# A Deltanet / RWKV-7 layer on one core: squares and column sums placed behind each convolution, and the memory rows' sum of squares placed after two of four RWKV units

## The chip, the cores and the metric

The kernel runs on one core of a Trainium2 chip. Its time is the device time of one execution in microseconds (us). Profiles are of one execution each. Engines are called TensorE (PE in the rows, with PEld for its weight loads), VectorE (DVE), ScalarE (ACT), GpSimd (POOL) and SyncE (SP), whose queue issues most DMA transfers.

## The reference, cut to what matters

One layer over 256 tokens of width 2048, all in fp32. It has three parts behind one another, each added to the residual: a mixer, an attention over 256 memory rows, and a squared-ReLU MLP with 8192 hidden units. The mixer is two groups side by side, Deltanet (8 heads of 128) and RWKV-7 (16 heads of 64).

```python
def l2norm(x):
    return x * lax.rsqrt(jnp.sum(x * x, axis=-1, keepdims=True) + 1e-6)

def deltanet_group(p, ...):
    qkv, z, ga, gb = jnp.split(p, ...)
    qkv = jax.nn.silu(causal_depthwise_conv(qkv, conv_w))
    q, k, v = ...                       # 8 heads of 128
    q = l2norm(q)
    k = l2norm(k)
    ...
    o = chunked_gated_delta_rule(q, k, v, g, beta)

def layer(h, mem, ...):
    p = rmsnorm(h, mix_norm_w) @ w_in
    o_dn = deltanet_group(p[..., :DN_COLS], ...)
    o_rw = rwkv7_group(p[..., DN_COLS:], ...)
    h = h + jnp.concatenate([o_dn, o_rw], axis=-1) @ w_out
    h = h + memory_cross_attention(rmsnorm(h, xa_norm_w), rmsnorm(mem, mem_norm_w), wq, wk, wv, wo)
    h = h + squared_relu_mlp(rmsnorm(h, ffn_norm_w), w1, w2)
```

## The kernel before

**The GEMMs.** Weights are read once, in blocks of 512 KB (`raw`, four buffers, loaded by SP). ScalarE rounds a block to its high half (`whi`, line 239), VectorE subtracts to get the low half (`wlo`, written through the helper at line 110), and TensorE multiplies high by high, low by high and high by low (lines 254, 255 and 257) into two of three PSUM banks `ps_g`, one for each half of the tokens. A block gives twelve matmuls of 512 columns. These three steps have a raised priority.

**The order of the work.** The body is written as a program; a planner orders each engine's instructions by priority and readiness, so that the small work of one part runs between the GEMM matmuls of the next. Each engine then runs its own list strictly in that order. Tiles of one tag share a fixed number of buffers, and a writer waits until a buffer of its tag is read for the last time.

**The first half of the program.** It is: the four RWKV units (`rk_group(u)`, before units 0 and 2 also `v_group(u)`, then `unit(u)`), then `dn_in(0)`, `dn_unit(0)`, `dn_in(1)`, `dn_unit(1)`, then `rms_dram` for the memory rows, the two `z` groups, and the GEMMs of the memory attention's keys and values. `rk_group`, `v_group` and `win_group` (three in each `dn_in`) are each a GEMM of 512 columns whose result goes from PSUM to a pair of `pt` buffers. The tag `pt` has four buffers; the loads of `rms_dram` (`junk`) use the same tag.

**RWKV and Deltanet units.** Unit `u` takes its small PSUM banks from stream `s0` or `s1` (two banks each), by `u % 2`; `dn_unit(g)` by `g`; the transposes of `dn_conv` and of the shifts use the one bank of stream `x`. Each unit forms small triangular matrices and inverts them: `inverse` writes them to DRAM (`scr`) and reads the diagonal blocks back (`g`), works on these on VectorE, writes them out and reads them back once more (`inv`, `xc`), and finishes with small matmuls of 32x32 and 64x64 elements.

**Deltanet's entry.** `dn_conv` transposes a `pt` pair, convolves on ScalarE and VectorE into `cy`, takes Tanh into `ct` (two buffers) and writes the SiLU's result, halves `q = 0, 1` one after the other. `dn_in(g)` does so for q, k and v of four heads. `dn_unit(g)` begins with the norms: ScalarE squares `kq` head by head into a `ct` buffer, TensorE sums the 128 channels by matmuls with a column of ones (line 865), and VectorE brings the sums to SBUF as `sk` (line 868), from which the scales of q, k and v follow.

**The memory rows.** `rms_dram` (lines 292 to 301) loads the 256 rows of `mem` in eight pieces of 256 KB, squares each on ScalarE with an accumulated row sum, and reduces the sums on VectorE; GpSimd takes the power. The result `rm` scales the keys and values of the memory attention.

Of the kernel before, what the change touches and what calls it, by code (L numbers as in the profile page):

```python
# [9 lines left out]
F32 = mybir.dt.float32  # L10
F32R = mybir.dt.float32r
AF = mybir.ActivationFunctionType
ALU = mybir.AluOpType
# [4 lines left out]
P = 128  # L18
D = 2048
S = 256  # L20
# [84 lines left out]
def body(ctx, tc, I, out, dbg=None, upto=99):  # L105
    nc = tc.nc
    V, A, G, T = nc.vector, nc.scalar, nc.gpsimd, nc.tensor
# [4 lines left out]
    def stt(o, a, s, b, op0, op1):  # L112
        return V.scalar_tensor_tensor(o, a, s, b, op0=op0, op1=op1)  # L113

    def ts(o, a, s1, op0, s2=None, op1=None, e=None):
        if s2 is None:
            return (e or V).tensor_scalar(o, a, s1, None, op0=op0)
        return (e or V).tensor_scalar(o, a, s1, s2, op0=op0, op1=op1)

    def act(o, a, f, scale=1.0, bias=0.0, accum=None):  # L120
        kw = {} if accum is None else {"accum_out": accum}
        return A.activation(o, a, f, bias=bias, scale=scale, **kw)  # L122
# [5 lines left out]
    const = ctx.enter_context(tc.tile_pool(name="const", bufs=1))  # L128
    small = ctx.enter_context(tc.tile_pool(name="small", bufs=2))
# [9 lines left out]
    def nm(s):  # L139
        cnt[0] += 1  # L140
        return f"{s}_{cnt[0]}"
# [3 lines left out]
    def bank(tag=None):  # L145

        if tag is None:
            tag = ("s0", "s1", "x")[cnt[0] % 3 if stream[0] is None else stream[0]]
        return ps.tile([P, 512], F32, tag=tag, bufs={"g": 3, "x": 1}.get(tag, 2), name=nm("ps_" + tag))
# [142 lines left out]
    def rms_dram(src, name):  # L292
        part = small.tile([P, 2, 4], F32, tag="ssp", name=nm("ssp"))
        for m in range(2):
            for q in range(4):
                junk = ptp.tile([P, 512], F32, tag="pt", name=nm("junk"))
                nc.sync.dma_start(out=junk, in_=src[:, m, 512 * q:512 * (q + 1)])
                act(junk, junk, AF.Square, accum=part[:, m, q:q + 1])
        ss = small.tile([P, 2], F32, tag="ss", name=nm("ss"))
        V.tensor_reduce(ss, part, axis=AX.X, op=ALU.add)  # L300
        return rms_end(ss, name)
# [482 lines left out]
    def win_group():  # L784
        pt = pts()
        gemm(xl, I["w_in"][gi[0]], NB, evac_tok(rx, pt))
        gi[0] += 1
        return pt
# [21 lines left out]
    def unit(u, rk_):  # L810
        stream[0] = u % 2
        rw_unit(u, rk_[0], rk_[1], vs[u])

    for u in range(4):
        t = rk_group(u)
        if u % 2 == 0:
            v_group(u)
        unit(u, t)
        if upto <= 1:
            return  # L820
    rps.close()
# [1 line left out]

    da = ctx.enter_context(tc.tile_pool(name="da", bufs=1, side="right", reuse_waits="tile"))

    def dn_conv(pt, j, g, dsts):
        for q in range(2):
            bb = bank()
            tpose4(bb, [pt[m][:, (2 * q + i) * P:(2 * q + i + 1) * P] for i in range(2) for m in range(2)])
            y = da.tile([P, 2, S], F32, tag="cy", bufs=2, name=nm("cy"))  # L830
            t = da.tile([P, 2, S], F32, tag="ct", bufs=2, name=nm("ct"))
            for i in range(2):
                blk = 8 * j + 4 * g + 2 * q + i
                src = bb[:, i * S:(i + 1) * S]
                act(y[:, i], src, AF.Copy, scale=C("conv", 4 * blk + 3))
                for s in range(1, 4):
                    stt(y[:, i, s:], src[:, :S - s], C("conv", 4 * blk + 3 - s), y[:, i, s:], ALU.mult, ALU.add)
            act(t, y, AF.Tanh, scale=0.5)
            stt(dsts(q), t, 1.0, y, ALU.add, ALU.mult)

    def dn_in(g):
        stream[0] = 2
        kq = da.tile([P, 4, 2, S], F32, tag="kq", bufs=2, name=nm("kq"))
        v2 = da.tile([P, 4, S], F32, tag="v2", name=nm("v2"))
        dn_conv(win_group(), 0, g, lambda q: kq[:, 2 * q:2 * q + 2, 1])
        dn_conv(win_group(), 1, g, lambda q: kq[:, 2 * q:2 * q + 2, 0])
        dn_conv(win_group(), 2, g, lambda q: v2[:, 2 * q:2 * q + 2])
        return kq, v2

    def dn_unit(g, kq, v2):  # L850
        def t4(tag, shape, bufs=1):
            pool = dns[0 if g == 0 and tag in ("Dm", "Bm", "At", "vt", "kt") else 1]
            return pool.tile(list(shape), F32, tag=tag, bufs=1 if tag != "ob" else 2, name=nm(tag))
# [1 line left out]
        stream[0] = g  # L855
        hd = slice(4 * g, 4 * g + 4)

        bs = bank()
        for i in range(4):
            sq = da.tile([P, 2, S], F32, tag="ct", bufs=2, name=nm("sq"))  # L860
            act(sq, kq[:, i], AF.Square)
            for j in range(2):
                for c in range(2):
                    o = j * 8 + c * 4 + i
                    T.matmul(bs[:, o:o + 1], lhsT=sq[:, j, c * P:(c + 1) * P], rhs=ones[:, 0:1],
                             start=True, stop=True)
        sk = small.tile([P, 16], F32, tag="sk", name=nm("sk"))
        ts(sk, bs[:, 0:16], 4e-6, ALU.add)
        s_ = small.tile([P, 2, 4], F32, tag="s_", name=nm("s_"))
        V.reciprocal(s_, sk[:, 0:8].rearrange("p (c h) -> p c h", c=2))  # L870
        tt(s_, s_, beta[:, :, hd], ALU.mult)
# [143 lines left out]
    Vm = late.tile([P, 2, NB], F32, name="Vm")  # L1015
    obs = [dn_unit(0, *kqv)]
    obs.append(dn_unit(1, *dn_in(1)))
    rm = rms_dram(I["mem"].rearrange("(m p) d -> p m d", p=P), "rm")
    z_group(0)
    z_group(1)  # L1020
    stream[0] = 2
# [217 lines left out]
```

## Time and profile before

| | us |
|---|---|
| three runs: median (lowest to highest) | 1428.85 (1423.86 to 1430.27) |
| the profiled execution, its own time | 1427.91 |
| its span in the profile | 1426.2 |
| TensorE busy, share of the span | 1407.6, 99% |
| VectorE busy | 945.7, 66% |
| ScalarE busy | 776.2, 54% |
| GpSimd busy | 53.0, 4% |
| mean granted TensorE clock, 1 being 2.4 GHz | 0.995 |

The span is the stretch from the first to the last instruction; 1.7 us of the execution's time lie around it. Busy times are unions, so matmuls that overlap in the array are counted once. Stretches of 5 or 10 us in the rows below give the clock that TensorE was granted as a share of 2.4 GHz; 0.50 is 1.2 GHz. In a timeline row the bracket gives how long the engine stood idle before the instruction and what ended the wait. Waits are put down to the last event that the profile shows.

### The profile page before, as it was taken

Reading aid. Unit: us, or ns where it says so; the run is one execution under the profiler, and the core shown is the slowest. Engines: PE = TensorE matmul, PEld = TensorE weight load, DVE = VectorE, ACT = ScalarE, POOL = GpSimd, SP = SyncE. Lnnn points to the kernel's source line nnn. Section 1 sums busy time; section 2 is a strip of 40 time slices with the busy share of each in tenths; the row PEclk is TensorE's granted clock in tenths of the full one; section 3 lists DMA queues with packets and bytes.
Section 4 is the critical chain, followed back from the end, with each engine's and each line's share of the span. In section 5 each row is a group of like instructions: output and inputs, shape, how many; then the busy total and the mean of one; then the engine's idle time right before and its main releaser. Section 6 shows DMA issues by size and latency. Waiting matters only on the chain.

```text
span 1426.2 us, 22860 instructions
## 1 busy us (share of the span) xinstructions
PE 1407.6 (99%) x8308; PEld 1172.1 (82%) x8308; DVE 945.7 (66%) x1788; ACT 776.2 (54%) x1476; POOL 53.0 (4%) x66
## 2 busy tenths in 40 slices
PE   9999999999999999999999999999999999999997
PEld 7877888788887878888788888888888888888886
DVE  7748563858688685766776555665556665566664
ACT  7655554455556454556765544555445544455553
POOL 0010001010010000000000000000000000000000
PEclk9999999999999999999999999999999999999999
DMA  7444443454358455555465566555665556655564
GB/s 272 160 154 142 137 130 106 136 195 140 105 186 238 141 170 173 177 177 178 140 200 189 187 191 198 186 187 192 192 193 191 189 188 194 194 185 188 192 192 148
DMA packets 90114, 250.80 MB, mean 176 GB/s; under 512 B 20609, under 2 KB 29329, under 8 KB 89617
## 3 DMA queue, kind: packets, MB, share of 16 engines
q1 hardware_dynamic: 69728, 241.86, 52.3%
q10 hardware_dynamic: 19920, 6.42, 1.9%
q8 instruction: 65, 1.06, 0.3%
q0 software_dynamic: 352, 1.06, 0.2%
q14 instruction: 49, 0.39, 0.1%
HBM read 242.62 MB, written 6.69 MB: 175 GB/s over the span
## 4 chain that ended last, share of the span: by engine, by line
PE 51%; issue 0%; ACT 0%; DVE 0%; POOLq 0%; POOL 0%
PE ps_g L278 17%; PE ps_g L281 9%; PE ps_g L255 8%; PE ps_g L254 8%; PE ps_g L257 8%; PE ps_g L223 0%; PE ps_g L225 0%; PE ps_g L224 0%; PE ps_x L320 0%; PE ps_s L320 0%; PE ps_s L1112 0%; ACT h L122 0%; ACT junk L122 0%; ACT whi L239 0%; POOLq L1235 0%
## 5 line engine op out<-in xcount | busy, mean ns | idle before, releaser
L110 DVE TENSOR_TENSOR wlo<-raw,whi 128x512 fp32r<-128x512 f32 x848 | 582.1, 691 | 366.6 <-ACT whi L239 314.2
L239 ACT CAST whi<-raw 128x512 fp32r<-128x512 f32 x848 | 524.0, 621 | 485.7 <-DVE wlo L110 202.6
L278 PE MATMUL ps_g<-hhl,whi 128*128 128x512 f32 x1088 | 297.3, 395 | 0.0
L254 PE MATMUL ps_g<-whi,xhl 128*128 128x512 f32 x512 | 207.4, 405 | 0.9 <-ACT whi L239 0.6
L278 PEld LDWEIGHTS ps_g<-hhl,whi 128*128 128x128 f32 x1088 | 186.7, 189 | 25.5
L255 PE MATMUL ps_g<-whi,xhl 128*128 128x512 f32 x512 | 204.1, 399 | 0.0
L254 PE MATMUL ps_g<-whi,fhi 128*128 128x512 f32 x480 | 186.8, 389 | 0.0
L255 PE MATMUL ps_g<-whi,flo 128*128 128x512 f32 x480 | 186.8, 389 | 0.0
L281 PEld LDWEIGHTS ps_g<-hhl,wlo 128*128 128x128 f32 x1088 | 166.3, 189 | 22.6
L281 PE MATMUL ps_g<-hhl,wlo 128*128 128x256 f32 x1088 | 172.9, 281 | 0.0
L257 PE MATMUL ps_g<-wlo,xhl 128*128 128x512 f32 x512 | 170.4, 405 | 2.1 <-DVE wlo L110 2.1
L257 PE MATMUL ps_g<-wlo,fhi 128*128 128x512 f32 x480 | 151.5, 389 | 0.0
L254 PEld LDWEIGHTS ps_g<-whi,xhl 128*128 128x128 f32 x512 | 97.2, 190 | 23.6 <-issue 1.7
L255 PEld LDWEIGHTS ps_g<-whi,xhl 128*128 128x128 f32 x512 | 97.1, 190 | 21.1 <-issue 2.2
L257 PEld LDWEIGHTS ps_g<-wlo,xhl 128*128 128x128 f32 x512 | 94.3, 190 | 23.8 <-DVE wlo L110 4.5
L255 PEld LDWEIGHTS ps_g<-whi,flo 128*128 128x128 f32 x480 | 90.1, 188 | 18.8
L257 PEld LDWEIGHTS ps_g<-wlo,fhi 128*128 128x128 f32 x480 | 90.1, 188 | 18.7
L254 PEld LDWEIGHTS ps_g<-whi,fhi 128*128 128x128 f32 x480 | 90.1, 188 | 18.5
L113 DVE SCALAR_TENSOR_TENSOR cy<-ps_x,colt,cy 128x255 f32<-128x255 f32 (+2 forms) x72 | 34.2, 475 | 2.8 <-ACT cy L122 2.1
L1205 ACT CAST fhi<-hid 128x256 fp32r<-128x256 f32 x64 | 26.1, 407 | 9.7 <-DVE hid L113 9.4
L113 DVE SCALAR_TENSOR_TENSOR h<-ps_g,rf,h 128x512 f32<-128x512 f32 (+1 forms) x34 | 22.9, 716 | 12.0 <-PE ps_g L225 8.7
L113 DVE SCALAR_TENSOR_TENSOR hid<-hid 128x256 f32<-128x256 f32 x64 | 27.3, 427 | 2.1
(353 smaller groups left out, 1440.2 us busy)
## 6 DMA issues: line engine op xcount, KB each, us to landing
raw<-in_w_dram SPq DMA_DIRECT2D x256, 512.0 KB, 4.2
raw<-in_w_in_dram SPq DMA_DIRECT2D x112, 512.0 KB, 3.5
raw<-in_w_out_dram SPq DMA_DIRECT2D x32, 512.0 KB, 4.3
raw<-in_wk_dram SPq DMA_DIRECT2D x8, 512.0 KB, 3.8
raw<-in_wv_dram SPq DMA_DIRECT2D x8, 512.0 KB, 3.5
raw<-in_wq_dram SPq DMA_DIRECT2D x8, 512.0 KB, 3.8
raw<-in_wo_dram SPq DMA_DIRECT2D x8, 512.0 KB, 3.5
wl<-in_w_lora_dram SPq DMA_DIRECT2D x8, 272.0 KB, 6.3
```

Of the source, the lines that this page charges most:

```text
L110: return (e or V).tensor_tensor(o, a, b, op=op)
L113: return V.scalar_tensor_tensor(o, a, s, b, op0=op0, op1=op1)
L239: A.copy(hi, w)
L254: T.matmul(acc[m][:, :n], lhsT=xh, rhs=w[q][0], start=first, stop=False)
L255: T.matmul(acc[m][:, :n], lhsT=xl, rhs=w[q][0], start=False, stop=False)
L257: T.matmul(acc[m][:, :n], lhsT=lhs(kb * KB + q, m)[0], rhs=w[q][1], start=False, stop=last)
L278: T.matmul(acc, lhsT=w[k][0], rhs=rhs(8 * b + k).rearrange("p a t -> p (a t)"), start=b == 0 and k == 0, stop=False)
L281: T.matmul(acc[:, 0:S], lhsT=w[k][1], rhs=rhs(8 * b + k)[:, 0], start=False, stop=b == 1 and k == 7)
L1205: A.copy(hi[:, j], t)
```

## The change

The squares and column sums of q and k are taken out of `dn_unit` and made in `dn_conv`, behind each half of the q and k convolutions. The Square goes into the `ct` buffer that held the Tanh, four sums go into a bank of the unit's own stream, and VectorE adds them to a tile `sk` that is kept for the whole kernel. The memory rows' `rms_dram` is called after `unit(1)` instead of after `dn_unit(1)`.

```diff
@@ the RWKV units @@
         unit(u, t)
+        if u == 1:
+            rm = rms_dram(I["mem"].rearrange("(m p) d -> p m d", p=P), "rm")
@@ dn_conv @@
-    def dn_conv(pt, j, g, dsts):
+    def dn_conv(pt, j, g, dsts, sums=None):
...
             act(t, y, AF.Tanh, scale=0.5)
             stt(dsts(q), t, 1.0, y, ALU.add, ALU.mult)
+            if sums is not None:
+                act(t, dsts(q), AF.Square)
+                bs = bank(f"s{g}")
+                for c in range(2):
+                    for i in range(2):
+                        T.matmul(bs[:, 2 * c + i:2 * c + i + 1], lhsT=t[:, i, c * P:(c + 1) * P], rhs=ones[:, 0:1],
+                                 start=True, stop=True)
+                ts(sums[:, :, 2 * q:2 * q + 2], bs[:, 0:4].rearrange("p (c h) -> p c h", c=2), 4e-6, ALU.add)
@@ dn_in @@
-        dn_conv(win_group(), 0, g, lambda q: kq[:, 2 * q:2 * q + 2, 1])
-        dn_conv(win_group(), 1, g, lambda q: kq[:, 2 * q:2 * q + 2, 0])
+        sk = const.tile([P, 2, 2, 4], F32, name=f"sk{g}")
+        dn_conv(win_group(), 0, g, lambda q: kq[:, 2 * q:2 * q + 2, 1], sk[:, 1])
+        dn_conv(win_group(), 1, g, lambda q: kq[:, 2 * q:2 * q + 2, 0], sk[:, 0])
...
@@ dn_unit @@
-        bs = bank()
-        for i in range(4):
-            sq = da.tile([P, 2, S], F32, tag="ct", bufs=2, name=nm("sq"))
-            act(sq, kq[:, i], AF.Square)
-            for j in range(2):
-                for c in range(2):
-                    o = j * 8 + c * 4 + i
-                    T.matmul(bs[:, o:o + 1], lhsT=sq[:, j, c * P:(c + 1) * P], rhs=ones[:, 0:1],
-                             start=True, stop=True)
-        sk = small.tile([P, 16], F32, tag="sk", name=nm("sk"))
-        ts(sk, bs[:, 0:16], 4e-6, ALU.add)
@@ before the z groups @@
-    rm = rms_dram(I["mem"].rearrange("(m p) d -> p m d", p=P), "rm")
     z_group(0)
```

## Rows read from the trace of the kernel before

**Rows 1.** The page, its first part: busy time, share of the span and instructions.

```profile
PE 1407.6 (99%) x8308; PEld 1172.1 (82%) x8308; DVE 945.7 (66%) x1788; ACT 776.2 (54%) x1476; POOL 53.0 (4%) x66
```

**Rows 2.** Long stretches: us, busy time of each engine, clock, DMA share, GB/s.

```profile
420.00:560.00 140.00, 136.95 (x1070) 110.28 (x1069) 106.46 (x232) 79.52 (x154) 9.64 (x6) 0.99 0.60 187
700.00:1410.00 710.00, 710.00 (x3607) 604.19 (x3606) 450.02 (x759) 373.77 (x671) 0.69 (x1) 1.00 0.59 191
1410.00:1426.20 16.20, 7.46 (x33) 5.81 (x31) 4.69 (x12) 4.50 (x12) 1.10 (x2) 0.85 0.36 130
```

**Rows 3.** Stretches of 5 us, same columns.

```profile
280.00:285.00 5.00, 5.00 (x14) 3.90 (x13) 1.53 (x2) 0.89 (x3) 0.64 (x1) 0.52 0.04 9
435.00:440.00 5.00, 3.97 (x18) 2.94 (x17) 2.98 (x10) 3.26 (x9) 0.00 (x0) 1.00 0.98 277
465.00:470.00 5.00, 5.00 (x90) 4.20 (x89) 1.78 (x5) 2.63 (x5) 0.00 (x0) 0.91 0.24 92
470.00:475.00 5.00, 5.00 (x51) 3.80 (x50) 1.12 (x2) 1.38 (x4) 0.00 (x0) 0.75 0.34 105
```

**Rows 4.** TensorE's timeline: start us, us, line, matmul, count, idle before.

```profile
88.81 0.60 PE L320 MATMUL ps_x<-cons,pt 128*128 128x128 f32 x4
...
118.29 0.60 PE L320 MATMUL ps_x<-cons,pt 128*128 128x128 f32 x4
...
276.20 0.70 PE L673 MATMUL ps_s<-IP,cons 128*128 128x256 f32 x2 [1.49 <-DVE IP L113]
...
434.40 0.71 PE L257 MATMUL ps_g<-wlo,xhl 128*128 128x512 f32 x2
434.95 0.40 PE L254 MATMUL ps_g<-whi,xhl 128*128 128x512 f32 x1
435.18 0.40 PE L255 MATMUL ps_g<-whi,xhl 128*128 128x512 f32 x1
...
438.44 0.73 PE L257 MATMUL ps_g<-wlo,xhl 128*128 128x512 f32 x2 [1.03 <-DVE wlo L110]
...
452.82 0.50 PE L257 MATMUL ps_g<-wlo,xhl 128*128 128x512 f32 x1 [0.61 <-DVE wlo L110]
...
466.33 1.95 PE L865 MATMUL ps_s<-cons,sq 128*128 128x1 f32 x16
...
470.47 0.63 PE L255 MATMUL ps_g<-whi,xhl 128*128 128x512 f32 x1
470.90 0.63 PE L254 MATMUL ps_g<-whi,xhl 128*128 128x512 f32 x1
```

**Rows 5.** VectorE's timeline.

```profile
350.89 0.68 DVE L110 TENSOR_TENSOR y<-y,ps_s 128x512 f32<-128x512 f32 x1
...
437.02 0.17 DVE L117 TENSOR_SCALAR x<-g 64x8 f32<-64x8 f32 x1 [2.83 <-DMA g<-scr]
```

**Rows 6.** What writes and reads the tile `sq`: its column sums.

```profile
L865 PE MATMUL ps_s<-cons,sq x64: 164/250/271, 371.3 to 473.8; 128*128 128x1 f32 x64
```

**Rows 7.** What writes the tile `sk`: duration min/median/max, first and last start.

```profile
L117 DVE TENSOR_SCALAR sk<-ps_s x2: 174/175/176, 381.7 to 476.1; 128x16 f32<-128x16 f32 x2
```

**Rows 8.** ScalarE's timeline.

```profile
108.34 0.68 ACT L122 ACTIVATE pt<-ps_g,rx 128x512 f32<-128x512 f32 x1
...
135.74 0.68 ACT L122 ACTIVATE pt<-ps_g,rx 128x512 f32<-128x512 f32 x1
...
336.87 0.61 ACT L122 ACTIVATE ct<-cy 128x512 f32<-128x512 f32 x1
...
446.40 0.19 ACT L122 ACTIVATION_READ_ACCUMULATOR junk<-junk 128x1 f32 x1
```

**Rows 9.** The timeline of SP's queue.

```profile
410.32 0.85 SPq L883 DMA_DIRECT2D Dm<-gc_dram  x2
...
422.39 0.85 SPq L297 DMA_DIRECT2D junk<-in_mem_dram  x2
```

**Rows 10.** A stretch of 10 us, columns as in rows 2.

```profile
110.00:120.00 10.00, 9.71 (x47) 7.88 (x47) 9.86 (x24) 5.51 (x10) 0.00 (x0) 1.00 0.50 155
```

More of the change, by code (lines that the diff above doesn't have):

```diff
@@ L844, in dn_in, with dn_unit @@
         v2 = da.tile([P, 4, S], F32, tag="v2", name=nm("v2"))
-        dn_conv(win_group(), 0, g, lambda q: kq[:, 2 * q:2 * q + 2, 1])
-        dn_conv(win_group(), 1, g, lambda q: kq[:, 2 * q:2 * q + 2, 0])
+        sk = const.tile([P, 2, 2, 4], F32, name=f"sk{g}")
+        dn_conv(win_group(), 0, g, lambda q: kq[:, 2 * q:2 * q + 2, 1], sk[:, 1])
+        dn_conv(win_group(), 1, g, lambda q: kq[:, 2 * q:2 * q + 2, 0], sk[:, 0])
         dn_conv(win_group(), 2, g, lambda q: v2[:, 2 * q:2 * q + 2])
-        return kq, v2
-    def dn_unit(g, kq, v2):
+        return kq, v2, sk.rearrange("p j c h -> p (j c h)")
+    def dn_unit(g, kq, v2, sk):
         def t4(tag, shape, bufs=1):
```

## The prediction

> **What bounds the kernel now.** I read the page first: TensorE is busy 1407.6 of 1426.2 us [rows 1]. All that a change could give back at full clock is the other 18.6 us. The stretches say where they lie: 8.7 us are in the last 16.2 us, where the output is normed and stored, and from 700 to 1410 us TensorE is never idle [rows 2]. So this change, which acts between 100 and 480 us, works on a few microseconds, and its number of matmuls stays what it is. The third view is the short stretches around Deltanet [rows 3], the fourth TensorE's timeline there [rows 4]. The reader is to see three things. (a) A pause of 1.03 us at 438.44 for a weight's low half from VectorE; VectorE stands 2.83 us at 437.02 for the transfer `g<-scr` [rows 5], in a stretch in which the DMA engines are 0.98 busy [rows 3]. (b) A pause of 0.61 us at 452.82, again for a low half. (c) From 465 to 475 us the granted clock is 0.91 and then 0.75 although TensorE is busy 5.00 of 5.00 us: by these rows 0.09 x 5 / 0.5 + 0.25 x 5 / 0.5 = 3.4 us at 1.2 GHz. In it matmuls of 512 columns start 0.43 us apart (470.47, 470.90) where they start 0.23 apart at 2.4 GHz (434.95, 435.18). Ahead of the fall stand 16 one-column sums in a row (466.33).
>
> **The change part by part, by what it adds or takes from TensorE's time.**
>
> *Squares and sums.* The count is unchanged: 64 one-column matmuls [rows 6] behind 8 Squares. What changes is where they stand. In the old place all four Squares of a group come behind the `v` convolution, since they take their buffer (`ct`) after it, and the sums stand in seven runs of 4 to 16, of which one is shown (466.33, [rows 4]). In the new place each half of the `q` and `k` convolutions is followed by four sums: 16 runs at most, so 9 more changes between plain and rounded matmuls. A change costs what the transposes show: the two matmuls behind them take 0.55 us (434.40 to 434.95) where two take 0.46, so 0.1 us. 9 x 0.1 = **+0.9 us** (0 where runs end beside other small matmuls).
>
> The evacuation of the sums becomes eight small VectorE instructions for two: 6 x 0.175 = 1.05 us [rows 7], spread over 100 us and hidden in VectorE's idle third. Were it all on the path it would be 1.05 us, which is its upper bound; I take 0.
>
> For the low clock I take **-1.5 us**: 3.4 us at half speed are worth at most 1.7, and the sums are the part of that stretch that goes; the lower bound is 0, if the rest of Deltanet's small matmuls does the same. The Trainium skill (TensorE: Matmul & The Clock Gate, "Why this matters for your kernels") says that idle gaps between bursts of matmuls are to be avoided, because the clock falls after them. The trace here shows the fall with no idle time in its two stretches; by the page nothing comes back from moving matmuls and the sum below would be 1428.1, by the row it is 1426.6.
>
> *What the sums now wait for.* They take a PSUM bank of stream s0 or s1, which RWKV units 2 and 3 use up to their last read; for unit 2 that is 350.89 [rows 5]. The `q` Squares therefore keep both `ct` buffers until some 352, and the first Tanh of the `k` convolution (now 336.87, [rows 8]) comes some 16 us later. Behind it on ScalarE's queue stand weight casts, but the order is dealt out anew with this wait known. Who needs `k`: `dn_unit(0)`, whose decay rows are only loaded at 410.32 [rows 9]. So 0, covered by those 50 us. By the same row group 0 gains nothing from earlier sums. Were the cover gone, `k`'s pair of `pt` would be held and the GEMM would stop: the first rival's mechanism. For group 1 the sums would be ready some 30 us before 476.1 [rows 7], and `dn_unit(1)`, which now sits in its chain Square, sums, Square, can go ahead.
>
> *The memory rows.* Eight loads of 256 KB, eight Squares, eight accumulator reads, one reduction and the power on GpSimd leave the stretch from 422.39 to 446.6 [rows 8, 9]. They add 2 MB to a stretch where the transfers are full, and the late `g<-scr` of (a) is what I read as their price: **-1.03 us** (0 if the weights alone fill the DMAs). Of (b) I take half, **-0.3 us** (0 to 0.61): VectorE's work there stays, only its lateness goes. In the new place the loads come behind `unit(1)` in the program. They depend on nothing but a `pt` buffer, yet in this trace they go out no earlier than 422, so buffers of a tag go out in program order; the new place is then between rk_group(1)'s pair (written at 108.34) and rk_group(2)'s (135.74) [rows 8]. DMA share from 110 to 120 is 0.50, so 2 MB fit, but VectorE is busy 9.86 of 10 us [rows 10], with unit 0's inverse and its transfers. The price is between 0 and what the old place cost, 1.64 us; I take **+0.6 us**, since the largest of those transfers is over by then. SP issues the loads among the weights' own: eight issues, 0.85 us for two [rows 9], against a weight block every 2.7 us (twelve matmuls of 0.23 us). GpSimd's power of `rm` has nobody waiting until the wk GEMM.
>
> *Sum:* -1.03 - 0.3 - 1.5 + 0.9 + 0.6 = -1.33. The profiled execution took 1427.91, so **1426.6 us**. It lies 0.9 us below the median of the three runs, 1428.85, which spread by 6.4. Bounds: all gains and no cost 1427.91 - 3.34 = 1424.6; no gain and all costs 1427.91 + 0.9 + 1.05 + 1.64 = 1431.5.
>
> **Rivals.**
>
> *Slower: the loads hold up rk_group(2).* They stand ahead of its pair of `pt`. With two buffers they took 24.2 us (422.39 to 446.6). v_group's pair is read by 89.4 [rows 4], so they can start at 109 and end at 133.2, 2.5 us before 135.74. If they start only when rk_group(1)'s pair is read, at 118.9 [rows 4], and keep that pace, they end at 143.1, 7.4 us late. Two of the three GEMM banks are then held, the next group lacks its second, and TensorE stops. Behind a stop there is low clock: the pause of 1.49 us at 276.20 [rows 4] is followed by a stretch at 0.52 [rows 3], 4.8 us at 1.2 GHz, worth 2.4. Time: 1426.6 - 0.6 + 7.4 + 2.4 = 1435.8. It decides once the last Square of the loads comes after 135.7. Against it: four buffers are free from 118.9, which should halve the time.
>
> *No change: the low clock isn't the sums' doing,* or comes back at another place of Deltanet's chain: 1426.6 + 1.5 = 1428.1. For it: 32x32 matmuls and the idle-gap rule of the Trainium skill (the page and section above; the trace agrees at 276.20, not at 465). Against it: the runs of sums are the longest small work in front of the fall.
>
> *Faster: the order of RWKV's second half changes too.* Everything behind rk_group(2) is dealt out anew, and the pause at 276.20 with its low clock (1.49 + 2.4 = 3.9) may go. With all gains and no cost: 1424.6 - 3.9 = 1420.7. For it: only that the pause comes from VectorE being late, which depends on the order. Against it: no operation of that unit changes.
>
> **How the numbers follow.** Half a per cent, 7.1 us, is about what a measurement of this kernel can tell from no change. The likeliest case has 0.56, the slower rival 0.14, the unchanged clock 0.16, the faster one 0.14. Faster by over 0.5%: 0.11 of the last and 0.03 of the likeliest's tail, 0.14. Slower: 0.10 and 0.03, 0.13. Within: 0.73. The likeliest's own range is 1424.6 to 1431.5; the range for 8 in 10 reaches past the two outer rivals' near sides, with the spread of the runs: 1419.5 to 1436.
>
> **What would show it.** Right: column sums in runs of four between the GEMM's matmuls from 350 on; no low clock around 470; the memory loads between 109 and 135 us with rk_group(2)'s evacuation still near 136; TensorE's idle time between 420 and 560 below its present 3.0 us [rows 2]; `dn_unit(1)`'s inverse earlier. Wrong: a pause of TensorE near 136 to 143, more low-clock time than now, or waits on the banks of s0 and s1 in front of the sums. The forecast fails most easily through order: a new order of 1,800 VectorE instructions can open pauses at places that no part of the change touches.

## The result and the profile after

| | before | after |
|---|---|---|
| median of the runs (lowest to highest), us | 1428.85 (1423.86 to 1430.76) | 1444.24 (1438.01 to 1449.77) |
| runs | 5 | 5 |
| the profiled execution: its time, its span | 1427.91, 1426.2 | 1438.01, 1436.3 |
| TensorE idle in the span (span less busy time) | 18.6 | 25.9 |

The ratio is 1.0106, 95% interval 1.0069 to 1.0144: the change makes the kernel slower by some 15 us, where 1426.6 us and no measurable change were forecast. The time lies outside the range, 1419.5 to 1436. In what follows one execution is left out of its ratio as disturbed: it took 1985.30 us at a mean clock of 0.652, in the kernel with one Square at the head.

The page of the changed kernel, its first part, answers to [rows 1]: TensorE does the same 8308 matmuls, and it is idle 7.3 us longer.

```profile
PE 1410.4 (98%) x8308; PEld 1174.6 (82%) x8308; DVE 947.0 (66%) x1794; ACT 776.2 (54%) x1476; POOL 55.2 (4%) x66
```

Where: first three stretches of the changed kernel, then two of the kernel before whose rows were not shown (its third is in [rows 2]). Columns as there.

```profile
100.00:150.00 50.00, 46.05 (x355) 34.84 (x354) 33.63 (x76) 29.82 (x67) 5.52 (x4) 0.97 0.57 184
...
345.00:420.00 75.00, 73.27 (x587) 61.21 (x587) 55.31 (x114) 39.97 (x75) 7.73 (x5) 0.98 0.39 128
420.00:560.00 140.00, 134.10 (x1068) 108.53 (x1067) 106.08 (x245) 69.62 (x131) 9.42 (x8) 0.99 0.50 157
```

```profile
100.00:150.00 50.00, 49.70 (x419) 39.00 (x418) 35.64 (x79) 30.76 (x67) 5.58 (x8) 1.00 0.51 152
...
345.00:420.00 75.00, 75.00 (x486) 63.35 (x485) 56.15 (x118) 41.58 (x77) 8.17 (x7) 1.00 0.43 140
```

The third column is TensorE's busy time. From 100 to 150 us, where the memory rows now are, it is idle 3.95 us for 0.30; from 345 to 420 us 1.73 for 0; from 420 to 560 us 5.90 for 3.05. These three make 8.2 us; the other stretches give 0.9 back. The clock falls in two stretches in which it was whole (0.97 and 0.98). The profiled execution is the fastest of the five; the others have less clock over the whole span (0.985, 0.989, 0.989 and one record of 0.944, against 0.993), so the median holds more low clock than this profile shows.

TensorE's timeline of the changed kernel, with its pauses and three of the six runs of sums:

```profile
129.01 0.38 PE L659 MATMUL ps_s<-cons,th 128*128 128x2 f32 x2 [2.58 <-ACT th L122]
...
353.01 0.63 PE L320 MATMUL ps_s<-cons,y 128*128 128x128 f32 x4 [1.73 <-DVE y L110]
...
360.27 1.28 PE L848 MATMUL ps_s<-cons,ct 128*128 128x1 f32 x10
...
367.61 1.95 PE L848 MATMUL ps_s<-cons,ct 128*128 128x1 f32 x16
...
437.68 1.84 PE L848 MATMUL ps_s<-cons,ct 128*128 128x1 f32 x16
...
449.12 0.73 PE L257 MATMUL ps_g<-wlo,xhl 128*128 128x512 f32 x2 [0.67 <-DVE wlo L110]
...
476.00 0.50 PE L254 MATMUL ps_g<-whi,xhl 128*128 128x512 f32 x1 [2.33 <-ACT whi L239]
...
505.14 1.02 PE L575 MATMUL ps_s<-Bm,Y 64*64 64x64 f32 x14 [1.20 <-ACT Y L572]
```

ScalarE's timeline behind two of them:

```profile
118.86 0.64 ACT L122 ACTIVATE junk<-junk 128x512 f32<-128x512 f32 x1 [1.40 <-DMA junk<-in_mem_dram]
...
125.86 0.63 ACT L122 ACTIVATE junk<-junk 128x512 f32<-128x512 f32 x1 [1.43 <-DMA junk<-in_mem_dram]
...
128.46 0.50 ACT L122 ACTIVATE th<-sh_k,colt 128x256 f32<-128x256 f32 x1
...
129.89 0.63 ACT L122 ACTIVATE junk<-junk 128x512 f32<-128x512 f32 x1
...
474.00 0.40 ACT L122 ACTIVATE b<-xc,cons 128x128 f32<-128x128 f32 x1 [3.16 <-DMA xc<-inv]
```

The pause at 129.01 waits for unit 1's `th`, and `th` stands on ScalarE's list behind Squares that wait for their loads. The pause at 476.00 waits for a weight's high half, which stands behind an operand of the inverse that comes back from DRAM. VectorE and SP of the changed kernel answer to [rows 5, 7, 9]:

```profile
441.46 0.21 DVE L117 TENSOR_SCALAR sk<-ps_s 128x4 f32<-128x4 f32 x2
...
448.26 0.17 DVE L117 TENSOR_SCALAR x<-g 64x8 f32<-64x8 f32 x1 [3.79 <-DMA g<-scr]
```

```profile
109.47 5.46 SPq L297 DMA_DIRECT2D junk<-in_mem_dram  x3
...
122.88 0.38 SPq L297 DMA_DIRECT2D junk<-in_mem_dram  x1
...
423.88 0.85 SPq L884 DMA_DIRECT2D Dm<-gc_dram  x2
```

Group 1's sums are ready at 441.5 us for 476.1, as forecast, and the memory loads go out at 109.5 to 122.9 us, as forecast. But VectorE's wait for `g<-scr`, put down to the memory loads that are now gone, is still there, and longer: 3.79 us for 2.83. The transfer itself is not longer. ScalarE's queue issues it; before, then after:

```profile
430.42 0.68 ACTq L490 DMA_DIRECT2D g<-scr  x1
```

```profile
444.36 0.65 ACTq L490 DMA_DIRECT2D g<-scr  x1
```

From issue to VectorE's reading it took 6.6 us before (430.42 to 437.02) and takes 3.9 us now (444.36 to 448.26). VectorE waits longer because its new list brings it there 0.1 us after the issue, and not 3.8.

### The profile page after: what moved, and what is told of

Its sections match the earlier page's. It is cut to its first block, busy times and chain, and to the rows that moved or that the text cites. A ratio compares the mean times of both kernels' runs of the same rounds, so it can differ in the third digit from the quotient of the medians.

```text
span 1436.3 us, 22858 instructions
## 1 busy us (share of the span) xinstructions
PE 1410.4 (98%) x8308; PEld 1174.6 (82%) x8308; DVE 947.0 (66%) x1794; ACT 776.2 (54%) x1476; POOL 55.2 (4%) x66
## 4 chain that ended last, share of the span: by engine, by line
PE 64%; ACT 1%; issue 1%; DMA 1%; DVE 0%; POOLq 0%; POOL 0%; ACTq 0%; DVEq 0%
PE ps_g L278 18%; PE ps_g L254 11%; PE ps_g L257 11%; PE ps_g L255 11%; PE ps_g L281 9%; DMA mraw<-in_memT_dram 1%; PE ps_s L320 0%; PE ps_g L223 0%; PE ps_g L224 0%; PE ps_g L225 0%; PE ps_x L320 0%; PE ps_s L936 0%; PE ps_s L942 0%; PE ps_s L575 0%; PE ps_x L1112 0%
## 5 line engine op out<-in xcount | busy, mean ns | idle before, releaser
L278 PEld LDWEIGHTS ps_g<-hhl,whi 128*128 128x128 f32 x1088 | 186.7, 189 | 25.5
L257 PEld LDWEIGHTS ps_g<-wlo,fhi 128*128 128x128 f32 x480 | 90.1, 188 | 18.9
L255 PEld LDWEIGHTS ps_g<-whi,flo 128*128 128x128 f32 x480 | 90.1, 188 | 18.6
```

What stands on the lines that cost most here:

```text
L255: T.matmul(acc[m][:, :n], lhsT=xl, rhs=w[q][0], start=False, stop=False)
L257: T.matmul(acc[m][:, :n], lhsT=lhs(kb * KB + q, m)[0], rhs=w[q][1], start=False, stop=last)
L278: T.matmul(acc, lhsT=w[k][0], rhs=rhs(8 * b + k).rearrange("p a t -> p (a t)"), start=b == 0 and k == 0, stop=False)
```

## The experiments

All kernels were timed beside the kernel before, whose medians in the five batches were 1427.71 to 1428.45 us. "Idle" is TensorE's idle time in the span of the profiled execution. The last column is the time that ScalarE and VectorE together stood idle for the transfer `xc<-inv` of the six inverses, from the view of the tile `xc`. "Places" compares TensorE's 8308 matmuls in the traces, in order of start: it is the number of positions at which a kernel has other tiles than the kernel before, tile numbers left out. (The expectations count by the planner's own list of 4652 entries, which no view shows; the figures differ.) A profile is of one execution: those of the sums alone and of the eight Squares added are the fastest of their twelve, that of the eight Squares at the head is the slowest of its five, and what is read from them leans that way.

| kernel | median us | ratio [95% interval] | idle us | places | `xc` wait us |
|---|---|---|---|---|---|
| before | 1427.7 to 1428.5 | 1 | 18.6 | 0 | 14.0 |
| after | 1444.24 | 1.0106 [1.0069, 1.0144] | 25.9 | 2634 | 18.9 |
| sums alone | 1430.99 | 1.0026 [1.0013, 1.0039] | 21.4 | 1385 | 12.3 |
| memory rows alone | 1441.3 | 1.0096 [1.0075, 1.0117] | 25.4 | 2250 | 23.6 |
| change, loads in buffers of their own | 1440.84 | 1.0097 [1.0079, 1.0114] | 25.6 | 2899 | 19.3 |
| rows behind unit 3 | 1427.28 | 1.0001 [0.9989, 1.0013] | 16.9 | 725 | 10.0 |
| eight Squares added | 1429.46 | 1.0019 [1.0007, 1.0031] | 19.0 | 1191 | 14.2 |
| eight loads added | 1431.83 | 1.0035 [1.0017, 1.0052] | 22.7 | 306 | 21.2 |
| sums of group 0 | 1435.23 | 1.0062 [1.0041, 1.0084] | 24.5 | 993 | 24.5 |
| sums, rows behind unit 3 | 1432.61 | 1.0036 [1.0022, 1.0049] | 21.3 | 1408 | 15.6 |
| loads and Squares, not tied | 1446.34 | 1.0123 [1.0102, 1.0143] | 28.0 | 2401 | 23.5 |
| rows, Squares later | 1439.48 | 1.0081 [1.0066, 1.0096] | 24.7 | 2740 | 25.5 |
| sums of group 1 | 1432.28 | 1.0044 [1.0026, 1.0063] | 22.1 | 910 | 22.4 |
| rows behind unit 2 | 1431.02 | 1.0022 [1.0008, 1.0036] | 19.5 | 748 | 11.6 |
| eight Squares at the head | 1445.08 | 1.0118 [1.0099, 1.0138] | 26.9 | 2317 | 25.1 |
| eight empty buffers | 1427.21 | 0.9993 [0.9980, 1.0005] | 19.8 | 92 | 12.5 |
| rows behind the first z group | 1428.96 | 1.0010 [0.9995, 1.0026] | 19.4 | 684 | 13.5 |
| one Square at the head | 1424.99 | 0.9983 [0.9972, 0.9993] | 16.5 | 288 | 9.4 |
| change, Squares at the head | 1439.61 | 1.0082 [1.0062, 1.0102] | 24.7 | 2929 | 19.1 |
| rows behind unit 3, one Square | 1425.13 | 0.9978 [0.9965, 0.9992] | 17.4 | 766 | 13.1 |

### One part of the change at a time

The sums alone (the change without the two lines of `rms_dram`) and the memory rows alone:

```diff
         unit(u, t)
+        if u == 1:
+            rm = rms_dram(I["mem"].rearrange("(m p) d -> p m d", p=P), "rm")
...
-    rm = rms_dram(I["mem"].rearrange("(m p) d -> p m d", p=P), "rm")
     z_group(0)
```

> Only the squares and column sums stand behind the convolutions; the memory rows keep their old place. Theory A (the loss comes from the memory rows, whose loads stop ScalarE in front of RWKV unit 1): the pause of 2.58 us at 129.01 is gone, and the time is that of the kernel before within 3 us, 1426 to 1432. Theory B (the loss comes from group 1's sums being early, which puts both of Deltanet's inverses into the same stretch): TensorE still pauses 2 to 3 us near 450 to 475 us, where the memory rows' late loads now stand as well, and the time is 1434 to 1444. Theory C (any new order loses): between 1430 and 1440, with pauses at other places.

> Only the memory rows move behind RWKV unit 1; squares and sums stay at the head of Deltanet's unit. Theory A: TensorE pauses by 2 to 3 us near 129 us waiting for ScalarE, low clock of 3.4 us behind it, and the time is 1433 to 1440, nearly all of the loss. Theory B: the pause near 129 is there but its price is given back by the late g<-scr of before being gone, so 1426 to 1431. Theory C: 1430 to 1440.

Measured: 1.0026 and 1.0096. The rows carry most of the loss: the pause near 129 us is gone with the sums alone and there with the rows alone (2.60 us at 129.04). Two stretches of the sums alone, to be held against [rows 3]:

```profile
465.00:470.00 5.00, 3.79 (x79) 2.86 (x78) 4.52 (x11) 3.35 (x7) 0.00 (x0) 1.00 0.29 105
470.00:475.00 5.00, 5.00 (x85) 4.06 (x85) 5.00 (x12) 1.28 (x3) 0.00 (x0) 1.00 0.60 213
```

The low clock of 465 to 475 us is gone in this profile, and TensorE lost 1.21 us there by standing still; over 420 to 560 us it is busy 132.91 us for 136.95. But that the moved sums took the low clock away is not shown. It is also gone in three kernels that keep all sums in the old place: the eight Squares added, the single Square, and the rows behind unit 3 with one Square. In the single-Square kernel the same run of 16 sums stands there, and behind it matmuls of 512 columns start 0.24 us apart, where they start 0.43 apart in [rows 4]:

```profile
467.18 1.95 PE L870 MATMUL ps_s<-cons,sq 128*128 128x1 f32 x16
...
470.45 0.40 PE L254 MATMUL ps_g<-whi,xhl 128*128 128x512 f32 x1
470.69 0.39 PE L255 MATMUL ps_g<-whi,xhl 128*128 128x512 f32 x1
```

With the sums of group 1 moved alone, on the other hand, the clock is 0.50 from 465 to 470 us.

Two stretches of the rows alone, one behind its pause at 129 us and one far from anything that was moved:

```profile
130.00:135.00 5.00, 4.30 (x13) 2.99 (x12) 5.00 (x13) 3.07 (x9) 0.00 (x0) 0.52 0.44 116
...
385.00:390.00 5.00, 5.00 (x19) 4.37 (x18) 2.01 (x6) 0.96 (x2) 2.51 (x2) 0.50 0.00 0
```

### The sums by group, and with the rows behind unit 3

```diff
-        dn_conv(win_group(), 0, g, lambda q: kq[:, 2 * q:2 * q + 2, 1], sk[:, 1])
+        dn_conv(win_group(), 0, g, lambda q: kq[:, 2 * q:2 * q + 2, 1], sk[:, 1] if g == 1 else None)
```

and likewise for `k`, with the old sums kept for the other group (`g == 0` in the other kernel); the third kernel has all sums behind the convolutions and `rms_dram` in front of Deltanet.

> Squares and sums behind the convolutions for group 0 alone; group 1 keeps them at the head of its unit, the memory rows their old place. If the small loss of the sums (1.0026) comes from group 1's unit starting early beside group 0's inverse: no loss here, 1425 to 1429. If it comes from the sums of group 0 waiting for a bank of stream s0 and standing in runs of 16: 1430 to 1433 here.

> The sums behind the convolutions for group 1 only; group 0 and the memory rows as before. Sums of both groups gave 1.0026 and of group 0 alone 1.0062. If the cost of the sums sits with group 0 (their wait for the bank of s0, and the order behind it), group 1 alone gives 0.998 to 1.001. If it is the two inverses that come to lie over each other once group 1's sums are early, 1.002 to 1.004. If each part only deals the order anew, anything within 0.997 to 1.006, with pauses at places that neither part touches.

> Squares and sums behind the convolutions for both groups as in the change, memory rows behind RWKV unit 3. If the two parts only add up: 1.0026 x 1.0001, 1430 to 1433, and no pause near 129 us. If the memory rows' late transfers near 440 were part of the sums' loss, since they meet both inverses there: 1425 to 1429.

Measured: 1.0062, 1.0044 and 1.0036, where both groups gave 1.0026. Each half costs more than the whole, and the first lies above both of its forecasts. Prices of this kind don't add, so none of them is the price of the sums.

### The memory rows taken apart

Added to the kernel before, behind unit 1: eight Squares of a resident tile into `pt` buffers, or eight loads without Squares; and, in the change, loads into eight buffers of their own:

```diff
...
+            for i in range(8):
+                junk = ptp.tile([P, 512], F32, tag="pt", name=nm("xsq"))
+                act(junk, cons[:, 0:512], AF.Square, accum=xpart[:, i:i + 1])
```

```diff
...
+            for i in range(8):
+                junk = ptp.tile([P, 512], F32, tag="pt", name=nm("xld"))
+                nc.sync.dma_start(out=junk, in_=mem_v[:, i // 4, 512 * (i % 4):512 * (i % 4) + 512])
```

```diff
+    mrow = [mm.tile([P, 512], F32, name=f"mrow{i}") for i in range(8)]
...
+        if u == 0:
+            for i in range(8):
+                nc.sync.dma_start(out=mrow[i], in_=mem_v[:, i // 4, 512 * (i % 4):512 * (i % 4) + 512])
...
-                junk = ptp.tile([P, 512], F32, tag="pt", name=nm("junk"))
-                nc.sync.dma_start(out=junk, in_=src[:, m, 512 * q:512 * (q + 1)])
+                junk = mrow[4 * m + q]
```

> The changed kernel, but the eight memory loads go into eight buffers of their own and are issued before RWKV unit 0, so that the Squares behind unit 1 never wait for a transfer. Theory A: the pause at 129 is gone and 4 to 6 us of the loss with it, so 1433 to 1439 beside 1444. Theory B: the stretch from 440 to 510 keeps its 4 us of pauses and its low clock; 1438 to 1446. If neither moves, the loss is the order's.

> The kernel before, memory rows in the old place, and eight extra Squares with row sums behind RWKV unit 1, of constants that are long in SBUF: ScalarE's work and the pt buffers of the move, without its transfers. Nothing reads them. If the move's price is ScalarE's work in front of unit 1's chain (1): a pause near 125 to 130 us and 1433 to 1440. If it is the transfers (2): no pause there and 1426 to 1431. If any new order of the stretch from 100 us on loses (3): 1432 to 1440 with pauses at other places as well.

> The kernel before, memory rows in the old place, and eight extra loads of 256 KB into pt buffers behind RWKV unit 1, without Squares: the transfers and the pt buffers of the move, without its work on ScalarE. Nothing reads them. (1) ScalarE's work is the price: 1426 to 1431. (2) the transfers are the price, by delaying unit 0's inverse and the weights: a pause near 125 to 130 us waiting for VectorE behind a late inv or xc, 1433 to 1440. (3) the order: little, since few instructions change places here, 1426 to 1431.

Measured: 1.0097, 1.0019 and 1.0035. The stretch of 100 to 150 us with the Squares, then with the loads:

```profile
100.00:150.00 50.00, 46.62 (x395) 35.59 (x394) 32.28 (x72) 29.99 (x70) 4.26 (x6) 1.00 0.46 142
```

```profile
100.00:150.00 50.00, 46.25 (x361) 35.41 (x360) 32.97 (x73) 24.83 (x52) 3.03 (x4) 0.97 0.57 175
```

Either of them, put between units 1 and 2, leaves TensorE idle for 3.4 to 3.75 us in that stretch, as the change does (3.95). The eight loads alone, which displace only 306 places, make TensorE pause at a transfer of the inverse, as their second forecast has it, though the time stays under its range. `xc<-inv` took 7.4 us from issue to landing there, for 4.7 at most before. TensorE, then VectorE:

```profile
133.82 0.73 PE L257 MATMUL ps_g<-wlo,xhl 128*128 128x512 f32 x2 [2.71 <-DVE wlo L110]
```

```profile
132.88 0.28 DVE L117 TENSOR_SCALAR b<-xc,cons 128x128 f32<-128x128 f32 x1 [3.42 <-DMA xc<-inv]
```

In the change with loads in buffers of their own, not only the loads moved: the planner put loads and Squares alike at 15 to 33 us. The stretch of 100 to 150 us then kept 49.14 busy us, and the loss was as large as in the change, at other places.

### Does ScalarE's wait for late loads make the difference?

The theory then was that the Squares are dear because they are tied to late transfers. One kernel has both additions untied; one has the moved rows with loads into their own buffers behind unit 1 and `rms_dram` behind unit 2; two have the rows as they are, one behind unit 2 and one behind unit 3.

```diff
...
+                junk = ptp.tile([P, 512], F32, tag="pt", name=nm("xld"))
+                nc.sync.dma_start(out=junk, in_=mem_v[:, i // 4, 512 * (i % 4):512 * (i % 4) + 512])
+                act(xscr, cons[:, 0:512], AF.Square, accum=xpart[:, i:i + 1])
```

> The kernel before with both halves of the memory rows' work added behind RWKV unit 1, but not tied to each other: eight loads of 256 KB of the memory rows into pt buffers, which nobody reads, and eight Squares of a resident tile into a scratch tile, so that no Square waits for a load. The old memory rows stay where they were. Squares alone gave 1.0019, loads alone 1.0035, the moved rows 1.0096. Theory A (the Squares' wait for late loads, in ScalarE's strict order, is the missing part): the two prices add, 1.004 to 1.0065, some 1434 to 1437 us, and no pause near 129 for th. Theory B (the sum of the work and a newly dealt order, with or without the tie): 1.008 or more, 1439 us and above. If it is A, the tie costs some 5 us; if B, none.

```diff
...
+        if u == 1:
+            for i in range(8):
+                nc.sync.dma_start(out=mrow[i], in_=mem_v[:, i // 4, 512 * (i % 4):512 * (i % 4) + 512])
+        if u == 2:
+            rm = rms_dram(mem_v, "rm")
```

> The memory rows alone (sums as before): the loads stand behind unit 1, as in the change, but into eight buffers of their own, and the eight Squares, the reduction and the power stand behind unit 2, by when the loads have landed; the old place is empty. Theory A (the tie): no pause near 129 us, and a ratio at or under that of the loads alone, 0.999 to 1.0035, since the loads of the old place are gone. Theory B (any new order in the RWKV units costs as much): 1.006 or more.

> The memory rows alone, behind unit 2: half a place later than in the change, half a place earlier than behind unit 3, where they cost nothing (1.0001). Theory A (the rows cost where ScalarE's list holds a unit's chain behind Squares that wait for transfers): unit 3 follows here as unit 1's chain did there, so 1.004 to 1.010 with a pause of TensorE or VectorE behind the Squares; behind unit 3 only a convolution of Deltanet follows. Theory C (only the place right behind unit 1, with the inverse of unit 0 in flight, costs): 0.999 to 1.003.

> The kernel before, with the memory rows alone moved, to behind RWKV unit 3 (ahead of Deltanet's entry), where VectorE and the transfers have most room (VectorE 3.5 to 3.8 of 10 us from 230 to 250). Theory A: no stop of ScalarE's chain, the late transfer of before is gone, 1424 to 1429, no slower than before. Theory C: slower by 3 to 10 us like any new order, 1431 to 1440.

Measured: 1.0123, 1.0081, 1.0022 and 1.0001. The first two kernels are no test of the tie, since the planner used the freedom that it was given. In the first the Squares stand at 18 to 33 us; in the second the view of the tile `mrow` has the loads and the Squares at the head, not behind units 1 and 2:

```profile
L823 SPq DMA_DIRECT2D mrow<-in_mem_dram x8: 328/328/435, 16.2 to 23.9; - x8
L122 ACT ACTIVATE mrow<-mrow x8: 614/626/629, 26.0 to 32.6; 128x512 f32<-128x512 f32 x8
```

What these two show is that a loss of this size comes without a Square that waits for a load between the units.

The third kernel lies under the forecast of the tie (1.0022 for 1.004 or more), and yet the pause of that forecast is there. ScalarE, then TensorE:

```profile
184.50 0.63 ACT L122 ACTIVATE junk<-junk 128x512 f32<-128x512 f32 x1 [2.19 <-DMA junk<-in_mem_dram]
...
185.13 0.35 ACT L724 COPY r<-ps_s 128x256 f32<-128x256 f32 x1
```

```profile
185.54 1.97 PE L727 MATMUL ps_s<-r,Sc 128*128 128x64 f32 x8 [2.91 <-ACT r L724]
```

TensorE waits 2.91 us for a copy that stands behind a Square that waited for its load, as it waits 2.58 us in the change; from 420 to 560 us this kernel is 2.34 us busier than the kernel before, which hides most of it in the ratio. So the tie has a price of 2 to 3 us of idle time where a unit's chain follows, and it is not the 15 us.

Behind unit 3 the move is free. Its stretch of 420 to 560 us:

```profile
420.00:560.00 140.00, 138.80 (x1070) 112.24 (x1069) 110.51 (x240) 77.07 (x141) 6.93 (x6) 0.99 0.53 177
```

1.85 us more busy time than in [rows 2], against 1.03 + 0.3 forecast. VectorE's wait for `g<-scr` and the pause behind it, for 2.83 and 1.03 us before:

```profile
437.96 0.17 DVE L117 TENSOR_SCALAR x<-g 64x8 f32<-64x8 f32 x1 [1.80 <-DMA g<-scr]
```

```profile
438.82 0.73 PE L257 MATMUL ps_g<-wlo,xhl 128*128 128x512 f32 x2 [0.21 <-DVE wlo L110]
```

The other pause, 0.61 us at 452.82, stays (0.62 us at 454.21). Most of the rest of the 1.85 us are two pauses of 0.59 and 0.53 us near 520 us in the kernel before, which the prediction does not name.

### The order without the work

In the untied kernel the Squares depended on nothing and stood at 18 to 33 us. So the same Squares were added alone, without any load. They write a scratch tile that nobody uses. Beside it stand three smaller disturbances: eight `pt` buffers taken and written in one column, the memory rows called one step later, and a single Square.

```diff
+        if u == 1:
...
+            for i in range(8):
+                act(xscr, cons[:, 0:512], AF.Square, accum=xpart[:, i:i + 1])
```

```diff
...
+                junk = ptp.tile([P, 512], F32, tag="pt", name=nm("xpt"))
+                V.memset(junk[:, 0:1], 0.0)
```

```diff
-    rm = rms_dram(I["mem"].rearrange("(m p) d -> p m d", p=P), "rm")
     z_group(0)
+    rm = rms_dram(I["mem"].rearrange("(m p) d -> p m d", p=P), "rm")
```

> The kernel before with eight Squares of a resident tile into a scratch tile added and nothing else: no loads, no pt buffers, sums and memory rows as before. They depend on nothing, so the planner puts them at 18 to 33 us on ScalarE, where TensorE waits for other things anyway. By order this kernel is the loads-and-Squares kernel (1.0123) without its loads: 768 of 4652 places in TensorE's order differ from the kernel before, only 39 from that kernel. Theory B (a newly dealt order costs, whatever the work): 1.006 to 1.011, with the pauses near 277 and 347 us that that kernel has. Theory A' (the loads, between units 1 and 2, do the harm through late transfers): 0.999 to 1.003, and neither pause.

> The kernel before with eight pt buffers taken behind unit 1 and written by VectorE in one column only: the turn of the pt buffers as in the change, without loads or Squares. The order hardly changes (41 of 4652 places on TensorE). Theory B: 0.998 to 1.002. A theory in which the turn of the pt buffers is the price: 1.004 or more with a pause behind an evacuation near 120 to 140 us.

> The kernel before with the memory rows called one step later, behind the first z group instead of in front of it: the same work at nearly the same time, and a new order in 287 of 4652 places on TensorE, all behind 330 us. If any new order costs: 1.001 to 1.004. If a small shift in time is free and the cost needs the RWKV units: 0.998 to 1.001.

> The kernel before with one Square of a resident tile added, 0.63 us on ScalarE at some 18 us, where it is idle. 97 of 4652 places in TensorE's order change. The work itself is worth nothing. If the price goes with the number of places that change: within 0.999 to 1.001. If one changed place near a transfer of an inverse is enough: 1.001 to 1.004, with a pause of over 1 us behind such a transfer.

Measured: 1.0118, 0.9993, 1.0010 and 0.9983. Some 5 us of work on ScalarE at the head, which nobody waits for, cost 17 us; the loads add nothing to that (1.0123). Where the Squares stand, TensorE's pause near 344 us, and VectorE's list ahead of it:

```profile
L122 ACT ACTIVATE xscr<-cons x8: 612/626/634, 18.8 to 32.9; 128x512 f32<-128x512 f32 x8
```

```profile
344.20 0.69 PE L740 MATMUL ps_s<-ze,Sc 128*128 128x64 f32 x2 [3.08 <-DVE ze L110]
```

```profile
338.92 0.29 DVE L117 TENSOR_SCALAR b<-xc,cons 128x128 f32<-128x128 f32 x1 [2.03 <-DMA xc<-inv]
...
343.73 0.41 DVE L110 TENSOR_TENSOR ze<-ps_s,nsg 128x256 f32<-128x256 f32 x1
```

TensorE waits for `ze`, which needs nothing of the inverse, but in the new order it stands on VectorE's list behind an operand of the inverse, and VectorE had stood 2.03 us for that operand's transfer. The kernel before has a longer wait for the same operand:

```profile
336.56 0.29 DVE L117 TENSOR_SCALAR b<-xc,cons 128x128 f32<-128x128 f32 x1 [2.49 <-DMA xc<-inv]
```

There `ze` was written at 331.76, in front of it, and TensorE paused only 0.39 us. So it is what stands behind a wait that made the difference here, more than its length. Two stretches of the kernel with the Squares, with less clock than before (1.00 and 0.99):

```profile
345.00:420.00 75.00, 75.00 (x538) 63.75 (x538) 48.70 (x98) 35.98 (x69) 7.74 (x5) 0.92 0.33 110
420.00:560.00 140.00, 133.66 (x982) 106.55 (x981) 104.34 (x238) 73.48 (x146) 11.23 (x9) 0.93 0.56 174
```

Two figures of the table go with the time. One is the number of changed places: the seven kernels with 2250 or more have ratios of at least 1.0081, the other twelve, with 1408 or fewer, at most 1.0062. The other is the wait for `xc<-inv`. The view of the tile `xc`, what its readers stood idle for (us, times): before, after, and the Squares at the head.

```profile
  DMA xc<-inv: 14.0, 10
```

```profile
  DMA xc<-inv: 18.9, 9
```

```profile
  DMA xc<-inv: 25.1, 10
```

In the table every kernel with up to 14.2 us of it has a ratio of at most 1.0026, and every one with 15.6 us or more at least 1.0035. Neither figure replaces the other: with a wait of 18.9 to 25.5 us the seven kernels with many changed places lose 0.8 to 1.2%, the three with 306 to 993 places 0.35 to 0.62%. These are correlations over 20 profiles; no run takes away this wait alone.

### The change in another order, and two favourable orders together

```diff
         unit(u, t)
+        if u == 0:
...
+            for i in range(8):
+                act(xscr, cons[:, 0:512], AF.Square, accum=xpart[:, i:i + 1])
         if u == 1:
             rm = rms_dram(I["mem"].rearrange("(m p) d -> p m d", p=P), "rm")
```

> The whole change, and the same eight Squares of a resident tile at the head: the work of the change with another draw of the order (506 of TensorE's places differ from the changed kernel, the last at some 340 us; behind that the order is the changed kernel's). If the loss is the moved work's own (the memory rows between units 1 and 2 late by their transfers): the pause near 129 us stays and the ratio is 1.009 to 1.013. If the loss up to 340 us is the draw: that pause goes or moves, and the ratio may come out anywhere from 1.004 to 1.014; what is behind 340 us stays, so not under 1.003.

> The best two draws together: the memory rows alone behind unit 3 (1.0001) and one Square of a resident tile at the head (0.9983), sums as before. If the gains of two draws add: 0.997 to 0.9995, some 1425 us. If every order is a draw of its own: 0.997 to 1.004.

Measured: 1.0082 and 0.9978. In the first the pause behind the memory rows is still there, at another place and on another operand; TensorE, then ScalarE:

```profile
126.67 0.50 PE L254 MATMUL ps_g<-whi,xhl 128*128 128x512 f32 x1 [2.03 <-ACT whi L239]
```

```profile
119.22 0.63 ACT L122 ACTIVATE junk<-junk 128x512 f32<-128x512 f32 x1 [1.97 <-DMA junk<-in_mem_dram]
...
125.39 0.63 ACT L122 ACTIVATE junk<-junk 128x512 f32<-128x512 f32 x1 [1.09 <-DMA junk<-in_mem_dram]
```

So a part of the loss belongs to the moved rows: 2.8 to 4.3 us of idle time between 100 and 150 us in each of the six kernels that have loads or Squares there, at most 1.34 us in the others. The second kernel has the lowest ratio of the study, 2.6 us under the kernel before by the medians, but it is within the interval of the single Square alone (0.9983): both of its theories allow it. Its stretch of 420 to 560 us:

```profile
420.00:560.00 140.00, 137.33 (x1069) 110.47 (x1068) 108.25 (x231) 75.26 (x138) 6.35 (x5) 1.00 0.55 177
```

## Why the prediction was wrong

**The memory rows at the new place, +0.6 us: the step that failed first.** The price was bounded by what the old place cost, 1.64 us. Measured in that stretch alone: 3.65 us more idle time and a clock of 0.97 over 50 us, 1.5 us, together 5.2 us. The bound looked at transfers, buffers and VectorE. The wait arose on ScalarE's list, which the prediction did not read at the new place: the Squares stand in its list among unit 1's and unit 2's own activations, and TensorE's next small matmuls need one of these (`th`). A wait of this kind, on this or another operand, is there in all four kernels whose Squares wait for their loads between two units (2.03 to 2.91 us).

**The sum had no term for the order.** It priced the instructions that move and left the rest where the trace of before has it. The last sentence on what would show it named a new order as the easiest way to fail, but the likeliest case got only 0.03 for slower, and the sum got nothing. Shown: an order of the same kind, dealt by eight Squares that nobody waits for, costs 1.0118 alone. The orders tried here ran from 0.9978 to 1.0123, and only two of 19 new ones were measurably faster than before. The span of a profile follows from TensorE's idle time and the granted clock: of the 10.1 us between the two spans 7.3 are idle time, and 2.8 are busy time, spent by the same 8308 matmuls at less clock (0.993 for 0.995). Which of the new pauses of the change come from the order, and not from the moved work, no run separates.

**The gains.** The pause of 438 us, -1.03: the reading was right. Where the rows alone leave, behind unit 3, the pause shrinks to 0.21 us. The pause of 452 us, -0.3: void, it stays at 0.62 us. That the stretch gained 1.85 us there is in part luck. In the change the gain is lost: the transfer is quicker (3.9 us for 6.6), but VectorE comes to it sooner and waits 3.79 us. The low clock from 465 to 475 us, -1.5: the step from the run of 16 sums to the fall behind it failed, since with the sums in the old place the clock was whole there in three kernels. In the change there is low clock from 475 to 480 us (0.77) behind the pause at 476.00. Group 1's sums came 34.6 us sooner, as said; its inverse then ran beside group 0's (its `scr` is written at 458.76, before group 0's `xc` is read back at 468.62; 31 us behind it in the kernel before), and VectorE and ScalarE wait for transfers there.

**Sums in 16 runs, +0.9: void.** They stand in six runs of 6 to 16, not in runs of four: one run fewer than before.

**The rivals.** The slower one had the right sign and the wrong mechanism: the last of the memory rows' Squares starts at 129.89, in front of its deciding point of 135.7, so `rk_group(2)` was not held up. The unchanged clock was right in that the low clock is not tied to the sums. The faster one needed the pause at 276.20 to go; in the change it is longer, 2.36 us at 288.20.

**What stays open.** How the 15 us divide between the moved rows' own price and the order is bounded only: eight Squares or eight loads at the new place cost 0.19% or 0.35% (2.7 or 5.0 us), each with a new order of its own in it. Where the low clock of the four slower executions of the changed kernel lies, no trace shows. That the wait for `xc<-inv`, or the number of changed places, causes the loss, rather than going with it, was not tried.

## What to carry to other kernels

Where a planner deals strict lists and the bound engine is busy for 99%, an edit also deals a new order to everything behind it, and here that was worth between -0.2% and +1.2%; give that order a range of its own, and measure it with an edit that adds only work nobody waits for, before a loss is put down to the edit. Read a pause back through the list of the engine that it names to the instruction that stood at a transfer, since the operand that TensorE lacks is often only queued behind it. Moved work belongs where no unit's chain follows it closely on the same engine: here behind the last unit, where it was free.

## What the hardware showed that was not expected

The small transfers of the inverses have no fixed time. `xc<-inv`, 64 KB, took 2.7 to 4.7 us from issue to landing before, 2.1 to 6.4 us with the Squares at the head, and up to 7.4 us with the eight loads added. The Trainium skill (DMA: Bandwidth & Descriptors, "Anatomy of one DMA — SWDGE (gpsimd) path") puts about 2 us of fixed time on a transfer of GpSimd's path, most of it the wait until the last byte is confirmed in memory. These transfers are issued by ScalarE; their lowest value, 2.1 us, is near that figure, and the highest is more than three times as much.

The clock was at 1.2 GHz for stretches in which TensorE was never idle (385 to 390 us with the memory rows alone: 5.00 of 5.00 us busy, clock 0.50), and it stayed whole in a stretch with 1.21 us of idle time (465 to 470 us with the sums alone). Idle time in a stretch did not tell, here, what clock it got.
